# An expert's products in one run of column halves, slot sums in PSUM, and gate and up rows in pieces of 4 KB

## Chip, cores and metric

The kernel runs on one core of a Trainium2 chip. The metric is the device time of one execution, in microseconds (us). Rows of the profile count from the start of the span, which is the time from the first to the last instruction of the profiled execution.

## The reference

256 tokens of width 1024 pass through two layers. Each layer has a mixer (gated linear attention in the first, differential attention in the second), a normalisation, a mixture of experts and another normalisation. Only the mixture of experts is touched by the change. Each token picks one of four groups and two of the group's four experts; an expert is a gated two-layer network of inner width 512:

```
combine = ...                      # (256, 16): weight of each expert for each token, mostly 0
for e in range(16):
    hdn = silu(t @ w_gate[e]) * (t @ w_up[e])      # 1024 -> 512
    y = y + combine[:, e:e + 1] * (hdn @ w_down[e])  # 512 -> 1024
```

All matrices are fp32. One expert has 2 MB of gate, 2 MB of up and 1024 x 512 x 4 bytes = 2 MB of down weights, 6.3 million bytes in all; 16 experts and two layers make 201 million bytes.

## The kernel before

**Tokens and slots.** `moe(layer, ...)` (line 469) gives each expert 64 slots. One-hot matrices (`one_hot`, tile OH) map tokens to slots for a group of four experts at a time. `gather_group` (line 536) multiplies the token rows `xa`, split into a high and a low part (`split_x`, line 527, tile xs), by the one-hot and so puts the slot vectors transposed into the tile xg: 128 partitions hold 128 features of one chunk k, for eight chunks; gain and bias of the normalisation are applied on the way out of PSUM (lines 553 to 560), from columns of the constant tile `pb`. Experts with more than 64 tokens are settled by one extra expert in layer 1 (so its loop has 17 turns, that of layer 0 has 16) and by a loop that runs only if still more are left (`overflow`).

**Products on column halves.** Slots are 64, so the stationary operand has 64 columns. `gu_part` (line 600) and `down_part` (line 629) issue the products in pairs, one on each half of TensorE's columns; the profile shows such forms as 128*64. An fp32 product is two instructions in the trace. Gate and up of one expert are 32 instructions (line 607), down is 16 (line 635). Everything else on TensorE uses the full width (128*128).

**One turn of the expert loop** (lines 762 to 790) issues on TensorE, in this order: the first quarter of gate and up of expert e (8 instructions); two transpositions of the hidden vectors of expert e-1 (`tr_part`, line 623); the second quarter (8); down of e-1 (16); two transpositions in `s_prep` (line 592), which turn the weighted one-hot of e around; the last two quarters (16); the scatter of e-1 into the four accumulators y (`scatter`, line 667, 4 instructions).

**Beside TensorE.** ScalarE takes silu (line 614) and VectorE the product with up (line 616) as soon as gate and up are done; VectorE copies the transposed hidden vectors (line 626); both take down's result out of PSUM into the tiles o (lines 643 and 644). For `s_prep` VectorE makes the weighted one-hot (line 589, tile ohw), compares the transposed one with zero (line 594, tile st), and ScalarE sums it into the slot weights `ws` (line 597), writing its unused output to an SBUF tile with the tag sl, which silu's output also has (one buffer). PSUM has two banks with the tag B (gate and up, half of down) and two with the tag C (the other half of down, all transpositions, gather).

**What sets the order.** A planner puts each engine's instructions in order, by priority of the program text and by its own estimate of when they are ready. `tc.issue_after(i)` adds that instructions of i's engine inside the block come behind i. `held` keeps the next group's one-hot and split behind the silu and product of experts 1, 5 and 9. In turn 5, `residual` and eight products with the identity (line 805) add the residual to y; they share the tiles o with down. At the start of a layer `combine` (line 563) is held behind the first one-hot.

**Weights.** `load_moe` (line 266) issues from SyncE's queue, six tiles of 1 MB per expert into a ring of 16 buffers and three spare ones. Tile j of the first four holds rows 256 j to 256 j + 255 of gate and of up, row 128 k + p in partition p: two pieces of 2 KB (one row each) for each partition and matrix. The down tiles have pieces of 4 KB (one row of 1024).

Of the kernel before, what the change touches and what calls it, by code (L numbers as in the profile page):

```python
# [20 lines left out]
S = 256  # L21
KC = D // 128
E = 16
# [20 lines left out]
def body(ctx, tc, x, w_in, wa_out, kv_w, wq, wb_out, wg, wu, wd, gate2, rows, rtab, lng, lnb, cblob, pblob, onehot, out):  # L44
# [39 lines left out]
    rw = const.tile([1, R_LAM], F32, name="rw")  # L84
    lnr = const.tile([64, 256], F32R, name="lnr")
# [237 lines left out]
    sp.dma_start(pb, pblob)  # L323
    sp.dma_start(rw, rows[0:1, 0:R_LAM])
# [144 lines left out]
    def moe(layer, M, lg, rstd, nr, fold, side=None):  # L469
        with tc.tile_pool(name=f"moe{layer}", bufs=1) as mp:  # L470
# [54 lines left out]
            gcol, bcol = P_G + 16 * layer, P_B + 16 * layer  # L525

            def split_x(k, eng, hold=None):

                t = mp.tile([128, 2, 2, 128], F32R, tag="xs", bufs=4, name=nm("xs"))
                x_ = xa[:, :, k * 128:k * 128 + 128]  # L530
                with after(hold):
                    act.activation(t[:, 0], x_, AF.Copy)
                eng.tensor_sub(t[:, 1], x_, t[:, 0])
                return t

            def gather_group(g, hold=None, xs=()):
# [7 lines left out]
                for k in range(KC):  # L544
# [7 lines left out]
                    for i in range(k, k + 1) if n == 5 else (k - 1, k) if k % 2 else ():  # L552
                        src = p[:, 0:256] if n == 5 else p[:, i % 2 * 256:i % 2 * 256 + 256]
                        gc, bc = (pb[:, c + i:c + i + 1] for c in (gcol, bcol))
# [30 lines left out]
            def s_prep(ohv, m, c_):  # L585
# [5 lines left out]
                for b in range(2):  # L591
                    pe.transpose(p[0:2 * m, b * 128:b * 128 + 128], w2[:, b].rearrange("p d s -> p (d s)"), ident)  # L592
# [5 lines left out]
                return st, ws  # L598
# [20 lines left out]
            def tr_part(h, nt, filler=0):  # L619
# [7 lines left out]
                return ht  # L627

            def down_part(wd_, ht, ws, nt, filler=0):
# [15 lines left out]
                return o  # L645
# [18 lines left out]
            def scatter(st, o, last, cols_first=False):  # L664
                for i in range(4):
                        b, c = (i % 2, i // 2) if cols_first else (i // 2, i % 2)
                        pe.matmul(y[b][c], st[:, b * 128:b * 128 + 128], o[c], start=False, stop=last, skip_group_check=True)  # L667
# [48 lines left out]
            def reload(ei, tile_, eng, et):  # L716
# [4 lines left out]
                for j in range(6):  # L721
                    t = tile_(j)
                    if j < 4:
                        t = t.rearrange("p (g k f) -> p g k f", g=2, k=2)
                        for gi, w in enumerate((wg, wu)):
                            eng.dma_start(t[:, gi], w[layer, bass.ds(ev, 1), j * 256:j * 256 + 256].rearrange("e (k p) f -> p (e k) f", p=128))
# [6 lines left out]
            def overflow(left, base, rev):  # L733
# [6 lines left out]
                st, wsx = s_prep(lambda b: oh[:, b], 64, cwx)  # L740
                p = pC()
                pv = p.rearrange("p (k s) -> p k s", k=KC)
                for k in range(KC):
                    for b in range(2):
                        pe.matmul(pv[:, k], xa[:, b, k * 128:k * 128 + 128], oh[:, b], start=b == 0, stop=b == 1)
                xg = mp.tile([128, KC, 64], F32, tag="o", bufs=2, name=nm("xgx"))
                gv, bv = (pb[:, c:c + KC].unsqueeze(2).broadcast_to([128, KC, 64]) for c in (gcol, bcol))
# [4 lines left out]
                ht = tr_part(act_part(p, 2), 2)  # L752
                scatter(st, down_part(wdn, ht, wsx, 2), True)
# [3 lines left out]
            hot = one_hot(0)  # L757
            gather_group(0, None, xs0)
            with tc.issue_after(hot.ins if hasattr(hot, "ins") else hot):
                cw = combine()  # L760
            prev = None
            for e in range(E + layer):
# [27 lines left out]
                prev = (h, *sp_)  # L790
# [22 lines left out]
            o = down_last(M[-1][1], tr_part(prev[0], 2), prev[2])  # L813
# [397 lines left out]
```

## Time and profile before

| what | us |
|---|---|
| three runs | 772.66, 772.68, 771.2; median 772.66 |
| the profiled execution's own time | 771.65 |
| its span | 770.0 |
| TensorE busy with products | 737.5 |
| VectorE busy | 362.3 |
| ScalarE busy | 297.2 |
| GpSimd busy | 8.9 |
| line 607 (gate and up), 1056 instructions | 261.4 |
| line 635 (down), 496 instructions on two banks at once | 112.9 |

The experts of layer 0 stand at about 137 to 367 us and those of layer 1 at about 510 to 757 us. 247.57 MB are moved, of which 244.68 MB by SyncE's queue. A row of the timeline gives the start, the time from the first start to the last end of instructions put together, the engine, the line, the operation, output and inputs, the shape and the count. Products are pipelined, so that the time from one row's start to the next row's start tells what a step costs, and the duration does not.

### The profile page before, as it was taken

The page shows a single profiled execution, that of the slowest core. Times are in us where ns is not written, and L with a number is a line of the kernel's source. Part 1 is how long each engine was busy: PE and PEld are TensorE (multiplying, and loading weights), DVE is VectorE, ACT ScalarE, POOL GpSimd, SP SyncE. Part 2 cuts the span into 40 slices and gives each one's busy share as a digit, 9 for nine tenths or more (in the row PEclk, how much of TensorE's full clock was granted, in tenths as well). Part 3 has the DMA queues.
Part 4 walks back from the last instruction along what each step waited for, and adds up shares of the span by engine and source line. Part 5 has one row for each costly group of instructions (what it writes and reads, how often), then busy time and mean ns, then how long its engine had stood idle before and what let it go on. Part 6 is the DMA issues. An engine that isn't in the chain of part 4 may idle for free. (4 is left out here: it accounts for less than half of the span.)

```text
span 770.0 us, 10596 instructions
## 1 busy us (share of the span) xinstructions
PE 737.5 (96%) x3743; PEld 397.0 (52%) x3743; DVE 362.3 (47%) x959; ACT 297.2 (39%) x651; POOL 8.9 (1%) x21
## 2 busy tenths in 40 slices
PE   7999998999999999999899999989999999999993
PEld 6898776434333434433698877743343243343331
DVE  3656766343173333322757877664235333232225
ACT  3554766333122322222756656552232233242123
POOL 1200000000000000000000000000000000000000
PEclk9999999999999999999999999999999999999997
DMA  7999856599999999999998346619999999999941
GB/s 227 315 380 389 328 205 254 200 396 393 381 387 393 395 395 393 393 392 358 289 372 326 110 146 237 217 63 386 394 385 395 393 391 391 396 394 392 393 160 56
DMA packets 131935, 247.57 MB, mean 322 GB/s; under 512 B 7932, under 2 KB 38117, under 8 KB 131750
## 3 DMA queue, kind: packets, MB, share of 16 engines
q1 hardware_dynamic: 131270, 244.68, 87.4%
q0 software_dynamic: 176, 1.59, 0.5%
q8 instruction: 31, 0.51, 0.3%
q10 hardware_dynamic: 432, 0.59, 0.2%
q14 instruction: 26, 0.21, 0.1%
HBM read 245.77 MB, written 2.63 MB: 323 GB/s over the span
## 5 line engine op out<-in xcount | busy, mean ns | idle before, releaser
L607 PE MATMUL pB<-W,xg 128*64 128x512 f32 x1056 | 261.4, 602 | 0.2
L607 PEld LDWEIGHTS pB<-W,xg 128*64 128x64 f32 x1056 | 69.8, 136 | 118.2 <-issue 111.5
L635 PE MATMUL pB<-W,ht 128*64 128x512 f32 x248 | 112.9, 594 | 0.0
L635 PE MATMUL pC<-W,ht 128*64 128x512 f32 x248 | 112.9, 594 | 0.0
L643 ACT ACTIVATE o<-pB,wst 64x512 fp32r<-64x512 f32 x31 | 21.1, 682 | 221.9 <-PE pC L635 208.6
L594 DVE TENSOR_SCALAR st<-pC 128x256 fp32r<-128x256 f32 x33 | 14.0, 425 | 160.6 <-PE pC L592 160.6
L119 DVE TENSOR_TENSOR lo<-W,hi 128x512 fp32r<-128x512 f32 x96 | 66.5, 696 | 37.4 <-PE pA L128 25.2
L118 ACT ACTIVATE hi<-W 128x512 fp32r<-128x512 f32 x96 | 59.3, 629 | 48.8 <-PE pA L129 28.3
L635 PEld LDWEIGHTS pB<-W,ht 128*64 128x64 f32 x248 | 33.3, 137 | 62.0 <-issue 59.8
L667 PE MATMUL pA<-o,st 128*128 128x512 f32 x132 | 40.2, 423 | 2.7 <-DVE o L661 2.1
L626 DVE COPY ht<-pC 128x256 f32<-128x256 f32 x33 | 14.0, 424 | 57.3 <-PE pC L623 57.2
L616 DVE TENSOR_TENSOR hd<-sl,pB 128x256 f32<-128x256 f32 x33 | 13.9, 421 | 56.7 <-ACT sl L614 56.7
L551 PE MATMUL pC<-OH,xs 128*128 128x256 f32 (+1 forms) x256 | 36.5, 292 | 3.6 <-DVE OH L519 2.2
L667 PEld LDWEIGHTS pA<-o,st 128*128 128x128 f32 x132 | 21.9, 188 | 33.6 <-issue 23.5
L551 PEld LDWEIGHTS pC<-OH,xs 128*128 128x128 f32 x256 | 32.9, 190 | 12.1 <-ACT xg L558 4.8
L129 PE MATMUL pA<-x1Thi,lo 128*128 128x256 f32 x128 | 36.1, 288 | 1.5 <-DVE lo L119 1.3
L635 PEld LDWEIGHTS pC<-W,ht 128*64 128x64 f32 x248 | 33.3, 137 | 7.0 <-issue 6.3
L127 PE MATMUL pA<-x1Thi,hi 128*128 128x256 f32 x128 | 36.7, 288 | 0.0
L128 PE MATMUL pA<-x1Tlo,hi 128*128 128x256 f32 x128 | 36.2, 284 | 0.0
L614 ACT ACTIVATE sl<-pB 128x256 f32<-128x256 f32 x33 | 12.7, 384 | 59.5 <-PE pB L607 59.5
L127 PE MATMUL pA<-hi,xThi 128*128 128x384 f32 (+1 forms) x96 | 34.6, 366 | 0.0
L128 PE MATMUL pA<-lo,xThi 128*128 128x384 f32 (+1 forms) x96 | 34.4, 358 | 0.0
(338 smaller groups left out, 1119.3 us busy)
## 6 DMA issues: line engine op xcount, KB each, us to landing
W<-in_moe_w_gate_dram SPq DMA_DIRECT2D x132, 512.0 KB, 10.9
W<-in_moe_w_up_dram SPq DMA_DIRECT2D x132, 512.0 KB, 10.8
W<-in_moe_w_down_dram SPq DMA_DIRECT2D x66, 1024.0 KB, 12.0
W<-in_a_w_in_dram SPq DMA_DIRECT2D x16, 256.0 KB, 6.1
W<-in_a_w_in_dram SPq DMA_DIRECT2D x4, 1024.0 KB, 17.0
W<-in_a_w_out_dram SPq DMA_DIRECT2D x4, 1024.0 KB, 14.9
W<-in_kv_w_dram SPq DMA_DIRECT2D x4, 1024.0 KB, 9.5
W<-in_b_w_q_dram SPq DMA_DIRECT2D x16, 256.0 KB, 5.4
```

Source lines behind the costliest of these rows:

```text
L118: act.activation(hi, src, AF.Copy)
L119: dve.tensor_sub(lo, src, hi)
L127: pe.matmul(o, l[0], r[0], start=first, stop=False, skip_group_check=skip)
L128: pe.matmul(o, l[0], r[1], start=False, stop=False, skip_group_check=skip)
L129: pe.matmul(o, l[1], r[0], start=False, stop=last, skip_group_check=skip)
L551: pe.matmul(o, xs[k][:, q // 2, q % 2], OH[g][:, q % 2].rearrange("p e s -> p (e s)"), start=q == 0, stop=q == 3)
L594: dve.tensor_scalar(st, p[0:2 * m, 0:256], 0.0, None, op0=ALU.is_gt)
L607: mm = pe.matmul(p[c * m:c * m + m, 0:2 * fw].rearrange("p (g f) -> p g f", g=2), xg(k), w[:, :, kk, c * fw:c * fw + fw], start=k == 0, st ...
L626: dve.tensor_copy(ht, pt[:, 0:n * 128].rearrange("p (c t) -> p c t", c=n))
L635: mm = pe.matmul(p[2 * c // nt][c * m:c * m + m, 0:w], ht[:, q % n, (q // n) * m:(q // n) * m + m], wd_[q // 2][:, q % 2, c * w:c * w + w] ...
L643: act.activation(hi, src, AF.Copy, scale=ws[a:a + m, 0:1])
L667: pe.matmul(y[b][c], st[:, b * 128:b * 128 + 128], o[c], start=False, stop=last, skip_group_check=True)
```

## The change

On TensorE a turn of the loop becomes: first quarter of gate and up of e (behind the transpositions of e-1), down of e-1, the other three quarters, and then at full width the scatter of e-1, the transpositions of `s_prep` for e and those of the hidden vectors of e itself, chained by `after`. The two line-594 and line-597 steps are held behind the product and the silu of the same expert, and the slot sums are written back into PSUM in place. The down products that follow take their transposed input from the turn before.

Gate and up rows are dealt to partitions as row 8 p + r, so that tile j holds rows 8 p + 2 j and 8 p + 2 j + 1: one piece of 4 KB for each partition and matrix. The features of xg must match, so `split_x` reads every eighth column of `xa`, and gain and bias come from a new tile `ngb`, loaded at the start by four small DMAs from GpSimd's queue. `combine` is held behind the fourth low part of the split instead of the one-hot.

```diff
+    ngb = const.tile([128, 2, 2, KC], F32, name="ngb")
...
-                        sp.dma_start(t[:, gi], w[layer, e, j * 256:j * 256 + 256].rearrange("(k p) f -> p k f", p=128))
+                        sp.dma_start(t[:, gi], w[layer, e].rearrange("(p r) f -> p r f", r=KC)[:, 2 * j:2 * j + 2])
...
+    for layer in range(2):
+        for c, w in enumerate((lng, lnb)):
+            pool.dma_start(ngb[:, layer, c], w[layer, 0].rearrange("(p r) -> p r", r=KC))
...
+            xa_r = xa.rearrange("p b (q r) -> p b r q", r=KC)
+            gbr = ngb[:, layer]
...
-                x_ = xa[:, :, k * 128:k * 128 + 128]
+                x_ = xa_r[:, :, k]
...
-                dve.tensor_scalar(st, p[0:2 * m, 0:256], 0.0, None, op0=ALU.is_gt)
+                with after(behind[1]):
+                    dve.tensor_scalar(st, p[0:2 * m, 0:256], 0.0, None, op0=ALU.is_gt)
                 ws = sm([128, 1], "wst")
-                jk = mp.tile([128, S], F32, tag="sl", bufs=1, name=nm("jk"))
-                act.activation(jk[0:2 * m], p[0:2 * m, 0:256], AF.Copy, accum_out=ws[0:2 * m])
+                with after(behind[0]):
+                    act.activation(p[0:2 * m, 0:256], p[0:2 * m, 0:256], AF.Copy, accum_out=ws[0:2 * m])
...
-            with tc.issue_after(hot.ins if hasattr(hot, "ins") else hot):
+            with after(lows[3]):
                 cw = combine()
...
                 p = pB()
-                mm = gu_part(M[e][0], (0,), xg, p, 2)
+                with after(prev and prev[4]):
+                    mm = gu_part(M[e][0], (0,), xg, p, 2)
                 if prev is not None:
-                    with tc.issue_after(getattr(mm, "ins", mm)):
-                        ht = tr_part(prev[0], 2)
-                mm = gu_part(M[e][0], (1,), xg, p, 2)
-                if prev is not None:
-                    with tc.issue_after(getattr(mm, "ins", mm)):
-                        o = down_part(M[e - 1][1], ht, prev[2], 2)
-                sp_ = s_prep(lambda b: OH[g][:, b, e - 4 * g], 64, cw[:, :, e] if e < E else extra[2])
-                gu_part(M[e][0], (2, 3), xg, p, 2)
-                if prev is not None:
-                    scatter(prev[1], o, False)
+                    with after(mm):
+                        o, mm = down_part(M[e - 1][1], ht, prev[2], 2)
+                with after(mm):
+                    mm = gu_part(M[e][0], (1, 2, 3), xg, p, 2)
                 h = act_part(p, 2)
+                with after(mm):
+                    if prev is not None:
+                        mm = scatter(prev[1], o, False)
+                    with after(mm):
+                        sp_ = s_prep(lambda b: OH[g][:, b, e - 4 * g], 64, cw[:, :, e] if e < E else extra[2], anchor)
+                    with after(sp_[2]):
+                        ht, mm = tr_part(h, 2)
...
-                prev = (h, *sp_)
+                prev = (h, *sp_, mm)
...
-            o = down_last(M[-1][1], tr_part(prev[0], 2), prev[2])
+            o = down_last(M[-1][1], ht, prev[2])
```

## Rows read from the trace of the kernel before

**Rows 1.** The page: TensorE's busy time, and its granted clock in 40 slices.

```profile
PE 737.5 (96%) x3743; PEld 397.0 (52%) x3743; DVE 362.3 (47%) x959; ACT 297.2 (39%) x651; POOL 8.9 (1%) x21
...
PEclk9999999999999999999999999999999999999997
```

**Rows 2.** Waits: who waited for what, us in total, times, longest.

```profile
PE pB L884 <- DMA scr<-in_cblob_dram: 4.9, 1, 4.9
```

**Rows 3.** Timeline of TensorE, one plain turn (start us, us, what, count).

```profile
267.90 1.94 PE L607 MATMUL pB<-W,xg 128*64 128x512 f32 x8
269.76 0.44 PE L623 MATMUL pC<-ident_r,hd 128*128 128x128 f32 x2
270.13 1.94 PE L607 MATMUL pB<-W,xg 128*64 128x512 f32 x8
...
275.44 0.44 PE L592 MATMUL pC<-ident_r,ohw 128*128 128x128 f32 x2
275.80 3.65 PE L607 MATMUL pB<-W,xg 128*64 128x512 f32 x16
279.39 1.20 PE L667 MATMUL pA<-o,st 128*128 128x512 f32 x4
280.52 1.07 PE L607 MATMUL pB<-W,xg 128*64 128x512 f32 x3
```

**Rows 4.** Timeline of TensorE: four transpositions together; a scatter before a gather.

```profile
89.34 0.60 PE L174 MATMUL pC<-ident_r,o_sb 128*128 128x128 f32 x4
...
249.09 1.20 PE L667 MATMUL pA<-o,st 128*128 128x512 f32 x4
250.12 2.06 PE L551 MATMUL pC<-OH,xs 128*128 128x256 f32 x16
252.18 1.07 PE L607 MATMUL pB<-W,xg 128*64 128x512 f32 x2
```

**Rows 5.** Timeline of VectorE and ScalarE in the same plain turn.

```profile
275.91 0.42 DVE L594 TENSOR_SCALAR st<-pC 128x256 fp32r<-128x256 f32 x1 [5.25 <-PE pC L592]
...
278.13 0.29 DVE L589 TENSOR_SCALAR ohw<-OH,comb 128x128 f32<-128x128 f32 x1
279.98 0.42 DVE L616 TENSOR_TENSOR hd<-sl,pB 128x256 f32<-128x256 f32 x1 [1.57 <-ACT sl L614]
...
279.56 0.38 ACT L614 ACTIVATE sl<-pB 128x256 f32<-128x256 f32 x1 [2.02 <-PE pB L607]
```

**Rows 6.** Timeline of ScalarE and VectorE behind the first expert of layer 0.

```profile
147.53 1.28 ACT L614 ACT_TABLE_LOAD   x1 [2.70 <-PE pB L607]
148.82 0.38 ACT L614 ACTIVATE sl<-pB 128x256 f32<-128x256 f32 x1
...
149.24 0.42 DVE L616 TENSOR_TENSOR hd<-sl,pB 128x256 f32<-128x256 f32 x1 [4.53 <-ACT sl L614]
```

**Rows 7.** Timeline of TensorE: the scatter in the turn behind the residual.

```profile
235.28 0.73 PE L667 MATMUL pA<-o,st 128*128 128x512 f32 x2 [0.29 <-DMA W<-in_moe_w_gate_dram]
```

**Rows 8.** Busy time by stretch (last: clock, DMA share, GB/s); one load's issue, landing, use.

```profile
338.80:349.60 10.80, 10.80 (x50) 3.72 (x48) 2.35 (x4) 2.34 (x5) 0.00 (x0) 1.00 1.05 391
349.70:355.10 5.40, 5.40 (x28) 1.85 (x26) 0.42 (x1) 0.00 (x0) 0.00 (x0) 1.00 1.03 402
...
327.01 0.44 SPq L282 DMA_DIRECT2D W<-in_moe_w_gate_dram  x1
...
W<-in_moe_w_gate_dram SPq DMA_DIRECT2D x132, 512.0 KB, 10.9
...
348.28 1.94 PE L607 MATMUL pB<-W,xg 128*64 128x512 f32 x8
```

**Rows 9.** Single lines (min/median/max ns): two VectorE sums over 160 elements.

```profile
L376 DVE TENSOR_REDUCE rsum<-wrg x2: 426/436/447, 22.0 to 30.3; 128x20 f32<-128x160 f32 x2
...
L497 DVE TENSOR_REDUCE rank<-cmp x2: 320/320/320, 131.0 to 503.9; 128x40 f32<-128x160 f32 x2
```

**Rows 10.** Timeline of GpSimd before its first wait ends.

```profile
9.69 0.21 POOL L681 TENSOR_SCALAR rev<-cb 128x16 f32<-128x16 f32 x1 [8.16 <-DMA cb<-in_cblob_dram]
```

More of the change, by code (lines that the diff above doesn't have):

```diff
@@ L524, in one_hot @@
                 return mm
-            gcol, bcol = P_G + 16 * layer, P_B + 16 * layer
+            xa_r = xa.rearrange("p b (q r) -> p b r q", r=KC)
+            gbr = ngb[:, layer]
+            lows = []
             def split_x(k, eng, hold=None):
                 t = mp.tile([128, 2, 2, 128], F32R, tag="xs", bufs=4, name=nm("xs"))
-                x_ = xa[:, :, k * 128:k * 128 + 128]
+                x_ = xa_r[:, :, k]
                 with after(hold):
                     act.activation(t[:, 0], x_, AF.Copy)
-                eng.tensor_sub(t[:, 1], x_, t[:, 0])
+                lows.append(eng.tensor_sub(t[:, 1], x_, t[:, 0]))
                 return t
@@ L553, in gather_group @@
                         src = p[:, 0:256] if n == 5 else p[:, i % 2 * 256:i % 2 * 256 + 256]
-                        gc, bc = (pb[:, c + i:c + i + 1] for c in (gcol, bcol))
+                        gc, bc = (gbr[:, c, i:i + 1] for c in range(2))
                         if n == 5:
@@ L581, in combine, with s_prep @@
                 return comb.rearrange("p b g e -> p b (g e)")
-            def s_prep(ohv, m, c_):
+            def s_prep(ohv, m, c_, behind=(None, None)):
                 w2 = mp.tile([128, 2, 2, m], F32, tag="ohw", bufs=2, name=nm("ohw"))
@@ L591, in s_prep @@
                 for b in range(2):
[L592 removed]
+                    mm = pe.transpose(p[0:2 * m, b * 128:b * 128 + 128], w2[:, b].rearrange("p d s -> p (d s)"), ident)
                 st = mp.tile([128, S], F32R, tag="st", bufs=2, name=nm("st"))[0:2 * m]
[L594 removed]
+                with after(behind[1]):
+                    dve.tensor_scalar(st, p[0:2 * m, 0:256], 0.0, None, op0=ALU.is_gt)
                 ws = sm([128, 1], "wst")
[L596 to L598 removed]
+                with after(behind[0]):
+                    act.activation(p[0:2 * m, 0:256], p[0:2 * m, 0:256], AF.Copy, accum_out=ws[0:2 * m])
+                return st, ws, mm
             def gu_part(ws, js, xg, p, nt):
@@ L626, in tr_part @@
                 dve.tensor_copy(ht, pt[:, 0:n * 128].rearrange("p (c t) -> p c t", c=n))
-                return ht
+                return ht, mm
             def down_part(wd_, ht, ws, nt, filler=0):
@@ L644, in down_part @@
                     dve.scalar_tensor_tensor(lo, src, ws[a:a + m, 0:1], hi, op0=ALU.mult, op1=ALU.subtract)
-                return o
+                return o, mm
             def down_last(wd_, ht, ws):
@@ L666, in scatter @@
                         b, c = (i % 2, i // 2) if cols_first else (i // 2, i % 2)
-                        pe.matmul(y[b][c], st[:, b * 128:b * 128 + 128], o[c], start=False, stop=last, skip_group_check=True)
+                        mm = pe.matmul(y[b][c], st[:, b * 128:b * 128 + 128], o[c], start=False, stop=last, skip_group_check=True)
+                return mm
             def blocks():
@@ L725, in reload @@
                         for gi, w in enumerate((wg, wu)):
-                            eng.dma_start(t[:, gi], w[layer, bass.ds(ev, 1), j * 256:j * 256 + 256].rearrange("e (k p) f -> p (e k) f", p=128))
+                            eng.dma_start(t[:, gi], w[layer, bass.ds(ev, 1)].rearrange("e (p r) f -> p (e r) f", r=KC)[:, 2 * j:2 * j + 2])
                     else:
@@ L739, in overflow @@
                     dve.tensor_scalar(oh[:, b], iota, q[:, b:b + 1], None, op0=ALU.is_equal)
-                st, wsx = s_prep(lambda b: oh[:, b], 64, cwx)
+                st, wsx, _ = s_prep(lambda b: oh[:, b], 64, cwx)
                 p = pC()
@@ L744, in overflow @@
                     for b in range(2):
-                        pe.matmul(pv[:, k], xa[:, b, k * 128:k * 128 + 128], oh[:, b], start=b == 0, stop=b == 1)
+                        pe.matmul(pv[:, k], xa_r[:, b, k], oh[:, b], start=b == 0, stop=b == 1)
                 xg = mp.tile([128, KC, 64], F32, tag="o", bufs=2, name=nm("xgx"))
-                gv, bv = (pb[:, c:c + KC].unsqueeze(2).broadcast_to([128, KC, 64]) for c in (gcol, bcol))
+                gv, bv = (gbr[:, c].unsqueeze(2).broadcast_to([128, KC, 64]) for c in range(2))
                 dve.tensor_mul(xg, pv, gv)
@@ L751, in overflow @@
                 gu_part(ws, range(4), lambda k: xg[:, k], p, 2)
-                ht = tr_part(act_part(p, 2), 2)
-                scatter(st, down_part(wdn, ht, wsx, 2), True)
+                ht, _ = tr_part(act_part(p, 2), 2)
+                scatter(st, down_part(wdn, ht, wsx, 2)[0], True)
             xs0 = [split_x(k, dve) for k in range(4)]
             act.activation(sm([128, 2], "warm"), xs0[3][:, 0, 0, 0:2], AF.Exp, scale=0.0)
-            hot = one_hot(0)
+            one_hot(0)
             gather_group(0, None, xs0)
-            with tc.issue_after(hot.ins if hasattr(hot, "ins") else hot):
+            with after(lows[3]):
                 cw = combine()
```

## The prediction

> **What bounds the kernel now.** I read the page first: TensorE is busy for 737.5 of 770.0 us and its clock is granted in full in every slice but the last [rows 1]. Busy is no proof of a bound, since products overlap, so the list of waits comes next: TensorE's only waits for a load are at line 884, in the first microseconds [rows 2]; in the expert loops it waits for nothing worth naming. The stretches show the second thing to watch: while the experts run, the DMA share is 1.03 to 1.05 at 391 to 402 GB/s [rows 8], so loads run at their limit too. One expert is 6.29 MB, 16.1 us at 391 GB/s, more than the 12.6 us of a plain turn below. The ring covers the difference, and its lead shrinks from turn to turn. The load of expert 15's first gate quarter is issued at 327.01; with the median 10.9 us to landing it is there at about 338, and is used at 348.28 [rows 8]: some 10 us of lead are left at the end of layer 0. So TensorE's stream of instructions is the bound, and the prediction is a count of that stream, with the loads as a ceiling to be checked.
>
> **One run of column halves.** A plain turn goes from 267.90 to 280.52: 12.62 us [rows 3]. Eight instructions of gate and up take 1.86 (267.90 to 269.76), sixteen take 3.59 (275.80 to 279.39). Eight more cost 1.73, so each run carries about 0.14 for entering and leaving the half-width form; the run from 270.13 to 275.44 (8 + 16 instructions, 5.31) agrees. The change makes one run out of three: 2 x 0.14 = 0.28 saved.
>
> **Full-width steps together.** The two pairs of transpositions take 0.37 (269.76 to 270.13) and 0.36 (275.44 to 275.80) [rows 3]. Four in a row span 0.60 where a pair spans 0.44 [rows 3, 4], 0.08 for each further one, so four should take 0.37 + 0.16 = 0.53: 0.20 saved (between none and 0.36, if the second pair were free). The scatter takes 1.13 before a half-width run (279.39 to 280.52) and 1.03 before full-width products (249.09 to 250.12) [rows 3, 4]: 0.10 saved. Together 0.58 per turn, and 12.04 for a plain one. There are 15 such turns in layer 0 (expert 1 on) and 16 in layer 1: **31 x 0.58 = 18.0 us.**
>
> **What this chain newly waits for in a plain turn.** The transposition of e's hidden vectors now follows its own silu and product instead of a quarter later. Scatter starts at 279.39, silu at 279.56, the product at 279.98 and it ends at 280.40 [rows 3, 5]: 1.01 behind the scatter's start. TensorE gets there after 1.03 of scatter and about 0.2 of `s_prep`: 1.23. About 0.2 us of cover; the next quarter and down are queued behind it, so whatever the product is late beyond that is lost on TensorE. The comparison st starts 0.47 behind its transposition (275.44 to 275.91) [rows 3, 5], hence at 1.5, ends at 1.9, and the slot sum in the same bank, of silu's size (0.38), at about 2.3 to 2.6. The next to need that bank is down, one quarter (1.7) behind the end of the transpositions at 1.56: 3.3. The copy of the hidden vectors ends by about 2.4, for the same 3.3. Both hidden, by 0.7 at least.
>
> **First expert of each layer.** It has no scatter to cover silu, and there silu needs a table load: 147.53 to 149.66 from the load's start to the product's end [rows 6]. Before, the next expert's quarter and more ran meanwhile; now this quarter is chained behind the transposition. ScalarE starts 0.17 behind the end of gate and up, as in the plain turn (279.39 to 279.56), so TensorE is free at 147.36, spends 0.2 on `s_prep`, and idles from 147.6 to about 149.7. **2 x 2.1 = 4.2 us lost.**
>
> **The turn behind the residual.** Down's result shares the tiles o with the residual's parts, and its scatter could not start before 235.28, after a gap of 0.29 [rows 7]: that turn ends with VectorE and ScalarE, and the 0.58 is not saved there: **1.2 lost** over two layers.
>
> **The six later gathers.** Scatter was followed by the gather at once, and a lone gate product of 1.0 us (252.18) stood between its halves [rows 4]. Now `s_prep` and the transpositions hold both C banks first; the gather's first bank comes free when the hidden vectors are copied, at about 2.4 behind the scatter's start against 1.56 for TensorE: 0.8 idle, about what the lone product costs now. Between -1.0 each (the lone product goes and nothing waits) and +1.0 (it stays too): -6 to +6. I take +0.2 each, **1 us lost**.
>
> **Split with a stride.** `split_x` now reads every eighth column. No row before shows this read. Nearest are two VectorE sums over 160 elements: 320 ns side by side, 436 ns with a stride of 32 elements [rows 9], 0.7 ns more for an element, 0.18 for a split of 256. There are 64 low parts and 64 high parts; if all of one engine's stood on the path, 64 x 0.18 = 11.5, if none, 0; nothing suggests a gain. Four low parts stand before the second half of a layer's first one-hot (0.7 for each layer), and the later ones mostly run behind products of experts 1, 5 and 9. **1.7 us lost**, near the low end for that reason. Here a rule speaks against the change: the Trainium skill, Advanced Engine Details and Errata, "SBUF Cachelines", says that SBUF is read in lines of 16 bytes and that a new line for each access costs extra. By it a stride of 32 bytes is as bad as that of 128 in the row, on both engines, and the sum would be nearer the upper end, 5 us more.
>
> **Pieces of 4 KB.** Gate and up in pieces of 2 KB move at 391 GB/s, down in pieces of 4 KB at 402 [rows 8]; at the second rate an expert's 4.19 MB take 10.4 instead of 10.7 us. TensorE does not wait for loads, so this is worth nothing by itself. It matters for the lead: by expert 15 TensorE is 14 x 0.58 - 2.1 - 0.6, some 5 us ahead of before, and about 5 of the 10 us of lead remain even if the loads gain nothing; with 0.3 for each of some twelve experts, 8 to 9. Value 0, bounds under the rivals. Four more issues on GpSimd fall into its 8.16 us of idle time before 9.69 [rows 10], which holds them at up to 2 us each; if they were later they would delay constants that nothing needs before the first mixer's end. `combine` changes place on VectorE within the first gather: 0, within half a microsecond.
>
> **Sum.** 18.0 - 4.2 - 1.2 - 1.0 - 1.7 = 9.9 us less than the profiled 771.65 (span 770.0 and 1.65 around it): 761.8. The median of the three runs, 772.66, is 1.0 above the profiled execution, so it may read up to 762.8; I say **762.0**.
>
> **Rivals.**
>
> *The product or `s_prep` comes late in every turn (slower).* The cover is 0.2 us. If VectorE had the two steps that weight the one-hot (0.29 each) behind the product instead of an expert ahead, `s_prep` would start 0.55 to 0.6 later in each of 31 turns: 17 to 18 us back, and with the other losses 771.65 + 8 = 780. It decides from 0.2 us of lateness on, and 0.5 us makes the change slower than before. For it: the transpositions are chained and nothing else can fill in. Against it: at 278.13 such a step runs before the product, far ahead of need [rows 5].
>
> *The loads become the bound (slower).* Partition p's piece now begins 16 KB behind that of p - 1, where before one tile's pieces were contiguous; no row shows such a step. If gate and up fell by a tenth, to 352 GB/s, an expert would take 1.2 us longer; over twelve experts 14, less the 5 of lead, 9 to 10 for each layer: about 781. It decides from a loss of 4% on. Beside it: the Trainium skill, DMA: Bandwidth & Descriptors, "Latency and other measured facts", reports half the rate at steps of 4 MiB and nearly the full one at 512 KiB, so that by the page 16 KB should be harmless; no run here shows it yet.
>
> *The clock falls in the idle 2.1 us (slower).* Rows show no fall: the gap before 235.28 is only 0.29 [rows 7]. If the next turn ran at 1.2 instead of 2.4 GHz, its half-width run of 10.4 us would take 10.4 more, twice: 783.
>
> *More goes than counted (faster).* If the lone products at the gathers go too and the residual's turn gets its 0.58: 6 + 1 + 1 = 8 more, 754. For it: chains leave the planner less room to split pairs. Against it: gather and residual are not in the chain.
>
> *It does half of what it says.* If four transpositions cost as much as two pairs and the stride its upper half, 31 x 0.20 + 4 = 10 less gain: 772, no change.
>
> **How the numbers follow.** Forecast 0.62, more goes 0.17, half 0.09, late product 0.06, loads 0.04, clock 0.02. The forecast's own range is 755 to 768. To leave out no more than 2 in 10 the range must reach to most of the faster rival, and to the edge of the half: 752 to 769. A change under 0.2% (1.5 us) cannot be told from none. Faster by more: 0.61 of the forecast, 0.17, and 0.05 of the half: 0.83. Within: 0.01 and 0.04: 0.05. Slower: 0.12.
>
> **What would show it.** Right: in a plain turn one run of 48 half-width instructions with 10.5 us to the scatter, the next such run 12.0 behind the last; four transpositions in a row, of which the third starts with no gap; silu's table load at the first expert with TensorE idle for about 2 us behind it, twice; clock still at full in all slices but the last; the down copy and the slot sum ending before down asks for them; GB/s in gate and up stretches at or above 391; no TensorE wait for a load. Wrong: gaps before line 623's transpositions in plain turns; gate and up loads below 375 GB/s with TensorE waiting for them; splits above 0.6 us; turns behind gathers longer by more than 1 us.

## The result and the profile after

The changed kernel takes **778.47 us** (median of 4 runs, 776.84 to 779.54) against 772.67 before: ratio 1.0072 [1.0057, 1.0088], slower by 5.8 us, where the prediction said 762.0. The profiled execution took 776.84 (span 774.9), 5.2 more than that of before; the sum had said 9.9 less, so 15.1 us have to be found.

The page, with the lines that answer to [rows 1] and the rates: TensorE is busy for 9 us less than before, in a longer span. PEclk, the granted clock of TensorE in tenths of full speed, is not full in slice 27, and several slices reach 409 and 410 GB/s.

```profile
PE 728.2 (94%) x3743; PEld 408.4 (53%) x3743; DVE 369.3 (48%) x959; ACT 311.2 (40%) x651; POOL 11.1 (1%) x25
...
PEclk9999999999999999999999999989999999999997
...
GB/s 217 312 387 401 332 204 234 187 410 409 331 399 409 378 410 409 410 409 338 290 391 248 110 170 211 217 29 390 409 326 410 410 364 383 410 408 409 409 148 55
```

So products became cheaper, as meant, and TensorE stands idle more. The list of TensorE's waits names the new idle time (who waited, for whom; us in total, times, longest). Behind the first microseconds no load is among them:

```profile
PE pC L559 <- DVE ht L635: 3.8, 6, 0.6
PE pC L559 <- DVE OH L523: 3.5, 2, 1.8
PE pB L616 <- DVE xg L568: 2.3, 5, 0.5
PE pC L559 <- ACT xg L566: 2.1, 4, 1.1
...
PE pA L676 <- DVE o L653: 2.1, 2, 1.1
PE pC L632 <- DVE hd L625: 1.8, 2, 0.9
...
PE pA L818 <- ACT res L815: 1.1, 2, 0.6
```

Line 559 is the gather, 616 gate and up, 676 the scatter, 632 the transposition of hidden vectors, 818 the residual's products. In the kernel before, the gather waited 2.2 for the one-hot and 1.3 for xg, and four of the seven lines did not exist:

```profile
PE pC L551 <- DVE OH L519: 2.2, 2, 1.1
PE pC L551 <- ACT xg L558: 1.3, 3, 0.6
```

The prediction says that TensorE waits for no load in the loops, while its row of 235.28 [rows 7] names one. The scatter reads no weights, and VectorE's last step on its first tile o ended at 235.22, so the reading of that gap by the tiles stands.

**The plain turn is right.** TensorE's timeline, one plain turn, against [rows 3]: one run of column halves from 272.39 to 282.84 (10.45 us; down stands between the two rows of line 616), then everything at full width; the next turn begins at 284.42. That is 12.03 us, where 12.04 was predicted, and nothing waits in it.

```profile
272.39 1.94 PE L616 MATMUL pB<-W,xg 128*64 128x512 f32 x8
...
277.59 5.32 PE L616 MATMUL pB<-W,xg 128*64 128x512 f32 x24
282.84 1.21 PE L676 MATMUL pA<-o,st 128*128 128x512 f32 x4
283.89 0.38 PE L600 MATMUL pC<-ident_r,ohw 128*128 128x128 f32 x2
284.11 0.38 PE L632 MATMUL pC<-ident_r,hd 128*128 128x128 f32 x2
284.42 1.94 PE L616 MATMUL pB<-W,xg 128*64 128x512 f32 x8
```

**Where it was lost.** The length of each turn, from the first gate product of one expert to that of the next, worked out from the profiled executions (us; "head" is the start of turn 0):

```
layer 0      head    0    1    2    3    4    5    6    7    8    9   10   11   12
before      136.7 10.5 13.5 12.6 14.6 15.7 13.3 19.0 16.2 15.7 12.6 12.6 17.3 12.6
changed     137.8 12.7 12.0 13.3 15.4 15.1 12.0 23.5 15.4 15.1 12.0 12.0 18.2 12.0
order_only  137.9 11.8 12.0 13.3 14.9 15.1 12.0 23.4 15.3 15.1 12.0 12.0 17.6 12.0
own_res     136.8 11.8 12.0 13.3 14.9 15.1 12.0 19.5 14.9 15.1 12.0 12.0 17.6 12.0
layer 1, turns 0 and 6: before 10.5 and 19.0; changed 14.4 and 22.6; own_res 12.0 and 19.5
```

Two places stand out: turn 6, behind the residual (+4.5 and +3.6), and the head with turn 0, where the split stands before the first gather.

The split, first before, then changed (line, count, busy us, mean ns of one): 0.20 more for each operation on VectorE, 0.27 on ScalarE.

```profile
L533 DVE TENSOR_TENSOR xs<-xa,xs 128x256 fp32r<-128x256 f32 x64 | 24.6, 419 | 7.7 <-ACT xs L532 7.2
L532 ACT ACTIVATE xs<-xa 128x256 fp32r<-128x256 f32 x64 | 23.8, 410 | 8.3 <-PE pC L551 7.1
```

```profile
L541 DVE TENSOR_TENSOR xs<-xa,xs 128x256 fp32r<-128x256 f32 x64 | 37.7, 621 | 8.9 <-ACT xs L540 8.9
L540 ACT ACTIVATE xs<-xa 128x256 fp32r<-128x256 f32 x64 | 39.7, 676 | 5.2 <-PE pC L559 4.9
```

Turn 6 of layer 0, first TensorE, then ScalarE. The residual goes through one pair of tiles o, one part after another: a copy (line 815), a subtraction on VectorE, two products (line 818), then the next copy. It began at 227.01 (before at 223.13), since VectorE now takes st, the hidden vectors' copy, the weighted one-hot and three low parts of the split ahead of the residual's rows, and each round waits for products that stand in TensorE's stream between gate and up. Down's result, finished at about 228.4, needs the same two tiles and leaves PSUM only from 237.50 (line 652); the scatter waits for it 1.05.

```profile
236.73 0.50 PE L818 MATMUL pA<-res,ident_r 128*128 128x512 f32 x1 [0.57 <-ACT res L815]
237.46 0.50 PE L818 MATMUL pA<-res,ident_r 128*128 128x512 f32 x1 [0.22 <-DVE res L816]
239.01 2.07 PE L676 MATMUL pA<-o,st 128*128 128x512 f32 x4 [1.05 <-DVE o L653]
240.88 0.63 PE L600 MATMUL pC<-ident_r,ohw 128*128 128x128 f32 x2
```

ScalarE, first before (one row), then changed:

```profile
223.13 0.63 ACT L802 ACTIVATE res<-xr 128x512 fp32r<-128x512 f32 x1 [6.16 <-DVE xr L424]
```

```profile
227.01 0.63 ACT L815 ACTIVATE res<-xr 128x512 fp32r<-128x512 f32 x1 [6.93 <-DVE xr L428]
231.43 0.63 ACT L815 ACTIVATE res<-xr 128x512 fp32r<-128x512 f32 x1 [3.79 <-PE pA L818]
...
236.06 0.62 ACT L815 ACTIVATE res<-xr 128x512 fp32r<-128x512 f32 x1
237.50 0.68 ACT L652 ACTIVATE o<-pB,wst 64x512 fp32r<-64x512 f32 x1 [0.82 <-DVE res L816]
```

In the scatter's row its four products stretch over 2.07 where the plain turn has 1.21: the clock had fallen. Busy time by stretch (from:to, length, then busy time with count of TensorE, its weight loads, VectorE, ScalarE and GpSimd, granted clock, DMA share, GB/s): the clock is at half, 1.2 GHz, from 136.1, from 238.5 and from 511.6, each time behind idle time of TensorE (1.72 at the head, then the waits above, then 1.76 at the head of layer 1). In the kernel before it fell only near the very end, as it does here too.

```profile
133.50:136.10 2.60, 0.88 (x7) 0.89 (x8) 1.97 (x6) 1.84 (x4) 0.00 (x0) 1.00 0.03 6
136.10:139.50 3.40, 3.40 (x11) 1.75 (x10) 2.91 (x6) 3.27 (x7) 0.00 (x0) 0.50 0.00 0
...
238.50:241.90 3.40, 2.89 (x10) 1.97 (x10) 1.56 (x3) 0.39 (x1) 0.00 (x0) 0.50 1.03 410
511.60:518.40 6.80, 6.48 (x24) 4.35 (x25) 4.55 (x15) 3.14 (x6) 0.00 (x0) 0.50 0.00 0
```

### The profile page after: what moved, and what is told of

It is laid out like the page before. It is cut to its first block, busy times and chain, and to the rows that moved or that the text cites. A ratio compares the mean times of both kernels' runs of the same rounds, so it can differ in the third digit from the quotient of the medians.

```text
span 774.9 us, 10566 instructions
## 1 busy us (share of the span) xinstructions
PE 728.2 (94%) x3743; PEld 408.4 (53%) x3743; DVE 369.3 (48%) x959; ACT 311.2 (40%) x651; POOL 11.1 (1%) x25
## 5 line engine op out<-in xcount | busy, mean ns | idle before, releaser
L616 PEld LDWEIGHTS pB<-W,xg 128*64 128x64 f32 x1056 | 77.2, 137 | 139.6 <-issue 130.0
L653 DVE SCALAR_TENSOR_TENSOR o<-pB,wst,o 64x512 fp32r<-64x512 f32 x31 | 23.1, 744 | 141.8 <-ACT o L652 141.8
L623 ACT ACTIVATE sl<-pB 128x256 f32<-128x256 f32 x33 | 12.7, 384 | 126.3 <-PE pB L616 126.3
L644 PEld LDWEIGHTS pB<-W,ht 128*64 128x64 f32 x248 | 33.2, 137 | 52.0 <-issue 48.3
L559 PE MATMUL pC<-OH,xs 128*128 128x256 f32 (+1 forms) x256 | 40.2, 309 | 9.5 <-DVE ht L635 3.8
L559 PEld LDWEIGHTS pC<-OH,xs 128*128 128x128 f32 x256 | 34.9, 203 | 21.4 <-ACT xg L566 11.2
L541 DVE TENSOR_TENSOR xs<-xa,xs 128x256 fp32r<-128x256 f32 x64 | 37.7, 621 | 8.9 <-ACT xs L540 8.9
L540 ACT ACTIVATE xs<-xa 128x256 fp32r<-128x256 f32 x64 | 39.7, 676 | 5.2 <-PE pC L559 4.9
L676 PEld LDWEIGHTS pA<-o,st 128*128 128x128 f32 x132 | 22.4, 191 | 33.3 <-issue 23.5
## 6 DMA issues: line engine op xcount, KB each, us to landing
W<-in_a_w_out_dram SPq DMA_DIRECT2D x4, 1024.0 KB, 14.4
```

Of the source, the lines that this page charges most:

```text
L541: lows.append(eng.tensor_sub(t[:, 1], x_, t[:, 0]))
L559: pe.matmul(o, xs[k][:, q // 2, q % 2], OH[g][:, q % 2].rearrange("p e s -> p (e s)"), start=q == 0, stop=q == 3)
L616: mm = pe.matmul(p[c * m:c * m + m, 0:2 * fw].rearrange("p (g f) -> p g f", g=2), xg(k), w[:, :, kk, c * fw:c * fw + fw], start=k == 0, st ...
L644: mm = pe.matmul(p[2 * c // nt][c * m:c * m + m, 0:w], ht[:, q % n, (q // n) * m:(q // n) * m + m], wd_[q // 2][:, q % 2, c * w:c * w + w] ...
L653: dve.scalar_tensor_tensor(lo, src, ws[a:a + m, 0:1], hi, op0=ALU.mult, op1=ALU.subtract)
L676: mm = pe.matmul(y[b][c], st[:, b * 128:b * 128 + 128], o[c], start=False, stop=last, skip_group_check=True)
```

## Experiments

Times are medians; ratios are to the kernel before, run on the same chip beside each (its medians lay between 772.6 and 772.7).

**1. The parts apart: order_only, flat_split, rows_only, fill9.**

order_only keeps the new order and the sums in PSUM, and takes the old rows, split and columns of gain and bias:

```diff
-    sp.dma_start(t[:, gi], w[layer, e].rearrange("(p r) f -> p r f", r=KC)[:, 2 * j:2 * j + 2])
+    sp.dma_start(t[:, gi], w[layer, e, j * 256:j * 256 + 256].rearrange("(k p) f -> p k f", p=128))
...
-    xa_r = xa.rearrange("p b (q r) -> p b r q", r=KC)
+    xa_r = xa.rearrange("p b (r q) -> p b r q", r=KC)
```

> The new order of the turn and the slot sums in PSUM, with the weight rows, the split and the gain and bias columns of before. Theory A (the strided split is what costs: 676 against 408 ns on ScalarE, 621 against 418 ns on VectorE, and with it the longer idle ahead of a layer's first gather, after which the clock fell): 764 to 768 us, no fall of the clock ahead of the first experts, plain turns at 12.0. Theory B (the order itself gives back what it saves, by waits for PSUM banks at the gathers and by the turn behind the residual): 772 to 775 us.

flat_split is the changed kernel with only the second of these two edits.

> The changed kernel with pieces of 4 KB, but the split reads 128 neighbouring columns, so the features of tokens and weights don't match and the result is another. Theory A: 764 to 768 us, as with the order alone, the splits back at 408 and 418 ns. Theory B: 775 to 778. If the pieces of 4 KB with their steps of 16 KB cost something by themselves, it stands above the order alone by that.

rows_only is the kernel before with the new rows, the strided split and ngb.

> The kernel before with the new rows of gate and up alone: pieces of 4 KB, the split with a stride, gain and bias from the new tile. Theory A: 776 to 781 us, slower than before by what the stride costs at the gathers, with the clock falling ahead of the first experts. Theory B: 772 to 774.

fill9 is the changed kernel with more zero products behind the rank sums:

```diff
-            warm(3, mm)
+            warm(9, mm)
```

> The changed kernel with nine instead of three products of zeros behind the ranks, in TensorE's idle time ahead of a layer's first gather. If the clock's falls at 136 us (3.4 us at half) and 512 us (6.8 us at half) come from that idle time of 1.7 us, they go, and 4 to 5 us with them: 773 to 775 us. If they come from something else, 778 to 780.

Measured: order_only 771.5, ratio 0.9983 [0.9973, 0.9993]; flat_split 770.8, 0.9979 [0.9969, 0.9989]; rows_only 781.03, 1.0103 [1.0088, 1.0118]; fill9 777.63, 1.0062 [1.0049, 1.0076]. The stride costs 7.7 us one way (changed less flat_split) and 8.3 the other (rows_only less before). But the order alone is worth 1.2 us, not 11 or so; its turn 6 takes 23.4 us in both layers. So there are two causes of nearly equal size. Pieces of 4 KB are worth nothing that shows (flat_split against order_only: the intervals overlap). Fill9 has no fall of the clock at the heads, and its turns 0 take 12.0 us in both layers for 12.7 and 14.4. Yet it gains only 0.8 us, within the intervals; its profile has falls at 239.0, 614.4 and 662.2 instead, of which the changed kernel's has only the first. So taking away the head's falls does not give the loss back; what they alone cost is not settled by it.

**2. Turn 6 and the banks: own_res, one_bank, own_bank, res_late.** All stand on order_only.

own_res:

```diff
-    hi, lo = (mp.tile([128, 512], F32R, tag="o", bufs=2, name=nm("res")) for _ in range(2))
+    hi, lo = (mp.tile([128, 512], F32R, tag="xs", bufs=4, name=nm("res")) for _ in range(2))
```

> The new order on the old weight rows (as order_only), and the residual's high and low parts in tiles of their own (the split's, four of them) in place of the two that the down product is evacuated into. Tile theory (turn 6 takes 23.4 us where the turn before takes 12.0, against 19.0 in the kernel before, because the residual and the down product of expert 5 take turns on two tiles, and the scatter behind the down product then waits 1.06 us for the evacuation): turn 6 falls to about 19 us in both layers, the waits of 0.57 and 1.06 us in it go, and the time falls by 6 to 9 us, from 771.5 to 763 to 766. Place theory (the turn is long because the residual's products fall among the pairs of column halves of the down product and leave both halves alone, whatever tiles they have): turn 6 stays at 22 us or more and the time within 2 us of 771.5.

one_bank:

```diff
-                pt = pC()
+                pt = pC() if bank is None else bank[:, 256:512]
```

> The new order on the old weight rows, and the one-hot's transpositions and those of the hidden values in one bank C (columns 0 to 255 and 256 to 511), so that the other bank is free for the gather that follows. Bank theory (the gather behind a turn waits 0.63 us because the two banks C hold the transposed one-hot and the transposed hidden values): the seven waits of 0.63 us ended by the copy of ht at 187, 253, 307, 360, 560, 625, 684 us go except where down_last itself needs ht (360, 753), which makes 5 to 6 times 0.63, 3 to 4 us, to 768. Rival (the wait is for something else that the copy orders, or is paid again in the slot sum and the transpositions sharing a bank): 771 to 772.5, and the plain turn grows above 12.0 us if the sharing costs anything.

> Both of the two edits. If they are independent, the gains add: 8 and 3.5 us, to about 760; if both only remove idle time behind which another wait stands, the time stays above 767.

res_late:

```diff
+                if e in (6, 7):
+                    with after(mm):
+                        mm = res_part(e - 6)
```

> Both edits, the residual's products placed behind the gate and up products of turns 6 and 7 (half of them in each) in place of among the down product's pairs, and seven in place of three zero products behind the rank sums at the head. Place theory: turns 6 and 7 together come to 12.0 + 12.0 + about 6 us for the residual's rows and products, 30 us where order_only has 38.7 and the kernel before 35.2, and the time falls to 756 to 760. Tile theory: no better than the same kernel without the new place (760). Head: the gap of 1.1 us before the first gather goes, and with it the clock fall behind it in the second layer (3.4 us at half clock, some 1.5 us).

Measured: own_res **763.37**, 0.9861 [0.9839, 0.9884]. Turn 6 is 19.5 us in both layers, and the waits in it are gone, although ScalarE begins the residual's copies later in the turn than in the changed kernel (226.65, 10.7 us into turn 6, against 8.7); TensorE's timeline of own_res there, with the scatter (line 672) right behind gate and up:

```profile
232.65 1.07 PE L612 MATMUL pB<-W,xg 128*64 128x512 f32 x2
233.65 0.50 PE L672 MATMUL pA<-o,st 128*128 128x512 f32 x1
233.99 0.39 PE L814 MATMUL pA<-res,ident_r 128*128 128x512 f32 x1
234.22 0.86 PE L672 MATMUL pA<-o,st 128*128 128x512 f32 x3
```

The tile theory holds: the late start alone does not make the turn long. The residual's products still stand among half-width ones, and turn 6 is short all the same, so the place theory does not explain the 4 us.

one_bank 799.48, 1.0355 [1.0337, 1.0373]; own_bank 794.0, 1.0296 [1.027, 1.0321]; res_late 791.02, 1.0235 [1.0214, 1.0255]. The shared bank was a mistake of mine, and an instructive one: both tiles are now one, and the program lets the transposition of the hidden vectors write it only behind the slot sum. TensorE waits for ScalarE in nearly every turn (29.2 us in 29 waits), here in one_bank; the plain turn is 13.4:

```profile
176.88 0.38 PE L596 MATMUL pC<-ident_r,ohw 128*128 128x128 f32 x2
178.40 0.44 PE L628 MATMUL pC<-ident_r,hd 128*128 128x128 f32 x2 [1.13 <-ACT pC L602]
```

That is the slower rival of the prediction made real: a step late by about 1.1 us in front of the chained transposition costs 28 us over the two layers. In their lists the gather's wait for the copy of the hidden vectors falls from six times to one, as the bank theory has it; of what that is worth their times say nothing. Only pairs with the same bank can be compared: one_bank less own_bank is 5.5 us for the tiles, own_bank less res_late 3.0 us for the residual's place and the fill together.

**3. Both causes on the changed kernel, and what is left: after_res, late_own, prep_early, steps.**

after_res is the changed kernel with own_res's edit.

> The changed kernel with one edit: the residual's high and low parts in the split's tiles in place of the two that the down product is evacuated into. If the two losses are independent (tiles of the residual: 8.1 us between order_only and own_res; stride of the split: 7.7 us between the changed kernel and flat_split), the time falls by 8 us from 778.5 to 770 to 771, which is just faster than the kernel before, and turn 6 falls from 23.5 and 22.6 us to about 19.5. Rival (the strided split runs on ACT and DVE in turn 6 too and becomes the next wait there): turn 6 stays above 21 us and the time above 773.

late_own is own_res with res_late's edit and `warm(7, mm)`.

> own_res (new order, old rows, residual in the split's tiles; 763.4 us), with the residual's products behind the gate and up products of turns 6 and 7, half in each, and seven zero products in place of three at the head. Place theory (products of 128 columns that fall among the pairs of column halves leave halves alone at 0.43 us where a pair takes as long): turns 6 and 7 fall from 19.5 + 14.9 to about 18.5 + 14 us, the gap of 1.1 us at the head to 0.55, together 3 us in two layers, to 760. Rival (what breaks the pairs is the broadcast rows of the residual, which stay): 762 to 764.

prep_early adds to it:

```diff
+    early = e in (3, 7, 11, 15)
+    mm = gu_part(M[e][0], (1, 2) if early else (1, 2, 3), xg, p, 2)
+    if early:
+        with after(mm):
+            sp_ = prep((None, None))
+        with after(sp_[2]):
+            mm = gu_part(M[e][0], (3,), xg, p, 2)
```

> late_own, and in turns 3, 7, 11 and 15 the one-hot's transpositions stand ahead of the last quarter of the gate and up products, with the comparison and slot sum waiting for nothing, as in the kernel before. Bank theory (the gather's 0.63 us wait ended by ht's copy is for one of the two banks C, both taken at the end of a turn): the waits at the gathers (186, 247, 301, 554, 616, 675 us) go or fall to 0.1, and 2.5 to 4 us with them, to 757. Rival (the transpositions alone, early, cost as much in the turn as they free: 0.2 us lone and a break of pairs each): no change from late_own.

steps splits blocks of k with `every(1, k)` to `every(8, k)`:

```diff
+    def every(n, k):
+        return xa[:, :, 0:128 * n].rearrange("p b (q r) -> p b r q", r=n)[:, :, k % n]
```

> order_only, and the split reads its 128 columns at a step of 1 (blocks 0 and 1), 2 (2 and 3), 4 (4 and 5) and 8 numbers of 4 bytes (6 and 7), each with a line of its own, so that features don't match the weight rows. Line theory (the page on cache lines: what counts is how many pieces of 16 bytes a row touches): 0.41 us at step 1, about the middle at step 2, and the full 0.62 to 0.68 us from step 4 on, with nothing more at step 8. Rival (a step of any size but one leaves a fast mode): 0.6 to 0.7 us from step 2 on. Second rival (price by distance): step 4 well below step 8.

Measured: after_res 768.77, 0.9968 [0.995, 0.9987], turn 6 at 19.5 in both layers: the two losses add, as if independent. late_own 760.4, 0.9839 [0.9825, 0.9853]; its turns 6 and 7 take 17.5 + 15.9 against 19.5 + 14.9, 1.0 less in each layer where 1.9 was expected, and the gap at the head is 0.55 for 1.1, twice. prep_early **757.69**, 0.981 [0.9798, 0.9823]. In own_res the six waits at the gathers stood in the list as

```profile
PE pC L555 <- DVE ht L631: 3.8, 6, 0.6
```

and in prep_early they are gone; the bank theory holds. What comes next shows in its list: for the first time gate and up wait for a load.

```profile
PE pB L612 <- DMA W<-in_moe_w_up_dram: 1.1, 1, 1.1
```

steps, a single execution (769.79), is told by its lines, by step 1, 2, 4 and 8, first ScalarE and then VectorE (mean ns behind the comma):

```profile
L541 ACT ACTIVATE xs<-xa 128x256 fp32r<-128x256 f32 x16 | 5.8, 408 | 0.1
...
L546 ACT ACTIVATE xs<-xa 128x256 fp32r<-128x256 f32 x16 | 6.0, 421 | 0.0
...
L551 ACT ACTIVATE xs<-xa 128x256 fp32r<-128x256 f32 x16 | 10.1, 670 | 3.6 <-PE pC L576 3.4
...
L556 ACT ACTIVATE xs<-xa 128x256 fp32r<-128x256 f32 x16 | 10.4, 659 | 0.0
```

```profile
L542 DVE TENSOR_TENSOR xs<-xa,xs 128x256 fp32r<-128x256 f32 x16 | 6.0, 416 | 0.0
...
L547 DVE TENSOR_TENSOR xs<-xa,xs 128x256 fp32r<-128x256 f32 x16 | 6.3, 415 | 0.0
...
L552 DVE TENSOR_TENSOR xs<-xa,xs 128x256 fp32r<-128x256 f32 x16 | 9.8, 611 | 7.0 <-ACT xs L551 7.0
...
L557 DVE TENSOR_TENSOR xs<-xa,xs 128x256 fp32r<-128x256 f32 x16 | 9.6, 637 | 0.4 <-ACT xs L556 0.4
```

None of the three expectations fits in full: a step of 2 is free, a step of 4 pays the whole price, and 8 no more.

**4. Pieces of 4 KB at a step of 2: pairs, pairs_best.** Partition q of tile j holds rows 256 j + 2 q and the next:

```diff
-    w[layer, e].rearrange("(p r) f -> p r f", r=KC)[:, 2 * j:2 * j + 2]
+    w[layer, e, j * 256:j * 256 + 256].rearrange("(p r) f -> p r f", r=2)
...
-    xa_r = xa.rearrange("p b (q r) -> p b r q", r=KC)
+    xa_r = xa.rearrange("p b (j q r) -> p b j r q", j=4, r=2)
```

> The changed kernel with its rows laid out in pairs: partition q of block j holds rows 256j + 2q and the next, so that a piece of gate or up rows is still 4 KB, but the split reads x at a step of 2 in place of 8. Step theory (what cost 7.7 us is the step of 8, not the 4 KB pieces): the split takes 0.41 us an operation as in the steps run, and the time falls to that of flat_split, 770.8 (769.5 to 772). Piece theory (some of the loss comes with the pieces in another way, as the four small loads of the gains and biases at the start or a memory pattern that the flat run did not disturb): 774 or more.

> prep_early (757.7 us) with gate and up rows in pairs, pieces of 4 KB at a step of 2. Its profiled execution waited 1.13 us for a load of up rows at 341 us, so TensorE comes near the loads there. Load theory (larger pieces land sooner: 409 against 391 to 393 GB/s in the slices between): the wait goes, 756 to 757 us. Rival (the pieces change nothing that binds): 757.4 to 758.2.

Measured: pairs 772.38, 1.0005 [0.9994, 1.0015], its split at a median of 431 and 418 ns; 6.1 us of the loss are back with the 4 KB pieces kept. It is 1.6 above flat_split, which the step theory does not give; in the profiled executions 1.4 of that lie before the first expert (138.4 against 137.0), and they are there by 22 us: ScalarE's first copy of the first mixer's weights waits for its load, which it does not do in flat_split (8.31) and the changed kernel (8.33).

```profile
9.11 0.63 ACT L119 ACTIVATE hi<-W 128x512 fp32r<-128x512 f32 x1 [0.71 <-DMA W<-in_a_w_in_dram]
```

At that time the four small loads of gains and biases are under way, now in pieces of 8 bytes instead of 32; the last lands at 9.3 instead of 8.0. pairs_best shows the same wait (0.77). That these loads are the reason was not tested apart. pairs_best 757.46, 0.9803 [0.9791, 0.9816]: the wait for a load is gone from its list, and the time is that of prep_early, as the rival had it. Both beat the kernel before by 15 us.

## Why the prediction was wrong, step by step

- **One run of column halves, and full-width steps together (18.0):** right in a plain turn, 12.03. Not every turn is plain: turns 1 and 2 of layer 0 saved 0.8 together (26.1 to 25.3), not 1.2.
- **What the chain waits for in a plain turn:** right; no wait in it, and one_bank shows what the cover of 0.2 us was worth.
- **The turn behind the residual (1.2 lost): failed.** The prediction saw that tiles o are shared and that VectorE and ScalarE end this turn, and took the turn's length of before as given. But down of expert 5 now stands a quarter earlier and the residual's rounds start 3.9 us later (1.4 of it the turn's own start), with more of TensorE's stream between them, so that down's result waits for the tiles until 237.50 and the turn is 4.5 and 3.6 us longer. The tiles cost 8.1 us by order_only and own_res, 9.7 by the changed kernel and after_res. Part of it is the clock: turn 6 is 23.4 or 23.5 where the clock falls well inside it and 22.5 or 22.6 where not (steps, and layer 1 of the changed kernel).
- **Split with a stride (1.7 lost): failed in its size.** 0.20 and 0.27 us an operation instead of 0.18, and 7.7 to 8.3 us in all, inside the bounds of 0 to 11.5, but not near the low end. (The medians of after_res and own_res differ by only 5.4; their ratios, which take in every execution, differ by 8.3 us, since those of after_res spread from 767.1 to 773.4.) What was foreseen came: 1.3 more for the one-hot at the two heads, where 0.7 for each was said. The prediction let products of experts 1, 5 and 9 cover the later splits; but a gather's last four parts are split while it runs, on both engines, and xg comes late: line 616 and the gather wait 2.3 + 2.1 for it against 1.3 before. Turn by turn against flat_split, 1.7 and 2.5 lie in the two heads with their turns 0, falls of the clock among them, and about 0.5 at each of the six gathers. The rule that spoke against the change was right: the Trainium skill, Advanced Engine Details and Errata, "SBUF Cachelines", has lines of 16 bytes and wants two hits on a line. The steps run agrees, with 408 and 421 ns on ScalarE at two or more numbers of 4 bytes from a line and 670 at one. The sum by that rule, 6.7 in place of 1.7, was 1.0 to 1.6 short.
- **First expert (4.2 lost):** too much. The table load no longer stands behind gate and up:

```profile
143.05 1.28 ACT L623 ACT_TABLE_LOAD   x1
148.86 0.38 ACT L623 ACTIVATE sl<-pB 128x256 f32<-128x256 f32 x1 [4.53 <-PE pB L616]
```

  In the kernel before [rows 6] ScalarE was idle for 2.70 as well, but the load waited with it: there a separate wait instruction (EVENT_SEMAPHORE, on ScalarE's sequencer ACTq) stood ahead of each silu and of the load. The changed kernel has none at its silu.

```profile
L614 ACTq EVENT_SEMAPHORE  x33: 17/17/17, 147.5 to 750.5; - x33
```

  That this comes of the slot sum's output, which shared silu's tile sl before, is likely and was not tested; rows_only, with the old slot sum, still has the wait (2.71), order_only has not. The load now ran during gate and up, and TensorE waited 0.90, not 2.1. In own_res turn 0 grew from 10.5 to 11.8 and 12.0: 2.8 for two layers. Of the 0.90, 0.4 are two steps of the weighted one-hot that VectorE ran ahead of the product, as in the first rival.
- **The six gathers (1.0 lost):** about right. The pairs of turns around them in layer 0 were 30.3, 31.9 and 29.9, and are 30.0, 30.0 and 29.6 in own_res: 2.5 saved, where 3 x (1.16 - 0.17) = 3.0 was said. The wait came as described (0.63), and prep_early gets 2.7 us by removing it.
- **Pieces of 4 KB (0):** right, and rate and step of 16 KB as hoped: 409 to 410 GB/s in full slices against 391 to 396 before. The stretch at 402 [rows 8] that the prediction read as down's held loads of the next mixer too, issued from 342.95 on. As a rival the loads played no part here; they came up at 757 us.
- **The clock rival (chance 0.02):** wrong in place and chance. It was looked for in the first expert's idle time; it fell behind the head's gap and in turn 6. Turn 0 was 12.7 and 14.4 with falls and 12.0 and 12.0 without them in fill9: with turn 6 some 4 us of the profiled execution. They stand behind idle time that the two causes made or lengthened, but falls come and go between executions, so that this share is an estimate.

The sum of the two failed terms: 8.1 at turn 6 and 6.0 to 6.6 at the split, 14 to 15 of the 15.1 us that were missing. That it fits so well is in part luck, since the first expert came out 1.4 better than said and some small losses were not foreseen. With both taken away (own_res) the kernel is at 763.4, near the 762.0, but own_res has no stride to pay: without the 1.7 the sum gives 760.1 for the profiled execution, which took 763.5. Of these 3.4, 1.0 is turn 6 (19.5 against 19.0) and 1.7 a turn of layer 1 behind a fall of the clock (13.7 against 12.0); what makes up the rest, and the 1.4 of the first expert, was not traced.

## What to carry to other kernels

Where a change moves a step ahead of another that uses the same buffers, follow the buffers and not only the engine: work out anew when each user of a shared tile starts and ends, above all in the one turn that is unlike the others. Price a strided read on every engine that makes it: here a step of 2 was free and steps of 4 and 8 cost the same on both engines, and rows laid out in pairs give the same large pieces as rows laid out in eights. On an engine that waits for nothing a small lateness in each turn adds up (1.1 us a turn made 28 us in one_bank), so a tile shared by two steps is to be counted as a wait until shown otherwise.

## What the runs showed of the hardware

- A read of 256 fp32 numbers in each of 128 partitions at a step of 2 took 421 ns on ScalarE and 415 on VectorE, as at step 1 (408 and 416); at steps of 4 and 8, 659 to 670 and 611 to 637 (steps).
- Gate and up rows in pieces of 4 KB came at 409 to 411 GB/s in full slices, with 16 KB from one piece to the next (changed kernel) and with pieces side by side (pairs); in pieces of 2 KB mostly at 391 to 396 (before).
- Inside the expert loops and at their heads TensorE's clock went to half for 3.4 or 6.8 us behind idle stretches of 0.5 to 1.8 us, in some executions and not in others: the gap of 1.15 at the head had no fall behind it in the profile of before, and one of 1.10 had one in order_only. In six of the traces it also went to half for 3.4 us at 32 to 33 us, in the first mixer, with no idle time of TensorE ahead of it (in order_only it was busy for 7.20 of the 7.20 us from 26.0 to 33.2); in the profile of before it did not.
- ScalarE's table load ran 5.8 us ahead of the silu that needs it where no wait instruction stood ahead of it (changed kernel, 143.05), and waited for gate and up together with the silu where one did (before, 147.53).
